# A transformer trunk on one core: units that keep three weight sums instead of two, and jobs that stand elsewhere in their stages

## The chip, the cores and the metric

The kernel runs on one core of one Trainium2 chip. The metric is the device time of one launch in microseconds, lower is better; the time before is the median of three runs. TensorE is called PE in the profile, VectorE DVE, ScalarE ACT, GpSimd POOL, and SyncE, which issues most loads, SP.

## The reference

Two layers work on 256 tokens of width 2048 in fp32. Each layer has a mixer (layer 0: neighbourhood attention with 16 heads; layer 1: a short gated convolution) and a gated MLP with a centred convolution of width 3 after the up projection (hidden width 5632).

```python
for i in range(DEPTH):
    a = rms_norm(h, mix_norm[i])
    if m == 0:
        mixed = neighborhood_attention(a, na_w_qkv[j], na_rpb[j], na_w_o[j])
    elif m == 1:
        mixed = short_conv_mixer(a, sc_w_in[j], sc_conv_w[j], sc_w_out[j])
    h = h + mixed
    h = h + conv_glu_ffn(rms_norm(h, ffn_norm[i]), ffn_w_up[i], ffn_conv_w[i],
                         ffn_conv_b[i], ffn_w_down[i])
return rms_norm(h, final_norm)

def conv_glu_ffn(x, w_up, conv_w, conv_b, w_down):
    h = dwconv_centered(x @ w_up, conv_w) + conv_b
    g, u = jnp.split(h, 2, axis=-1)
    return (jax.nn.silu(g) * u) @ w_down
```

## The kernel before, in words

**Precision.** Every fp32 operand is split into a high part (a cast, `hi`, made by ScalarE in `high_part`, L189) and a low part (the difference, `lo`, made by VectorE in `low`, L192). A product is the sum of high x high, low x high and high x low, so each weight has to be loaded, cast and subtracted before TensorE can use it.

**Stages.** The program is a list of items, each with its chunks of weights (`chunks`; a chunk is at most 128 x 1024 fp32, 512 KB). `prep_to` keeps four items' worth ahead: it loads a chunk into one of six `raw` buffers, casts it and subtracts. There are four kinds of stage:

- `Phase` (query and key, up projections, the convolution mixer's input): an item is usually two tiles of 128 output features. Its four chunks feed 32 matmuls of 512 columns on the high parts (L266) and 32 of 256 columns on the low parts (L274). Each tile is then evacuated. In an up projection that is: copy (ACT, L319), add (DVE, L320), scale (L325), convolution (ACT L333, DVE L335 twice), gate (ACT L739 or DVE L742), split for the next product (ACT L298, DVE L299). At some tiles the sums of activations for a unit are made as well (`make_forms`: POOL L520 to L523, then `split_into`, whose casts carry L298 and write `sf` and `act`).
- `Values`: the attention's value projection (L683 to L685). Between the items stand the scores (`scores`, L611 to L613 on PE, the softmax on DVE and ACT, L626 its last step) and the transposes of the probabilities (`probs`, L636).
- `Tokens` (attention output, the four half down projections, convolution output): groups of four output blocks; the weights come in pairs i, in an order written out by hand (`plan`). A pair marked P is eight products. A pair marked H is a unit: seven products (`seven`, L461 on; each product is the three matmuls L457 to L459), after Strassen. These seven need sums of weights, and their results are put together at the end of a group (`combine`, L487 on).

**Sums of weights.** The sums of a unit that can be made early are made by a job (`make`, L197) in an earlier stage: it loads three 256 KB pieces into activation tiles that are still free (the first two jobs of a stage allocate three each, later jobs alternate between the two sets), adds them on DVE (L212, L213) one chunk later, and stores the results to DRAM from ACT's queue (L218) three chunks later. Before, two sums per unit are kept. At use, `prep_to` loads them (512 KB, kind "kept"), casts them, and makes the other two sums with two dependent adds in `pair_of_sums` (L168, L169), of which the first reads the cast's source; the cast of the result waits for them.

**What sets the order.** A scheduler orders each engine's instructions at build time; each engine then runs its list in order. `load` (L157) chains every load on SP behind the one before through `newest["SP"]`, jobs' loads too. Where jobs stand is set by `QK_JOBS`, `V_JOBS`, `UP_JOBS` and `SC_JOBS` (how many per stage) and by L245 (between which items of a phase: from a fifth of the items, where the phase has introductory items, otherwise from the first, up to the share `until`).

## Time and profile before

| what | before |
|---|---|
| median of three runs | 2274.24 us (2273.21 to 2274.66) |
| the profiled execution, its time | 2272.17 us |
| its span | 2270.4 us |
| PE busy | 2205.6 us (97%) |
| DVE busy | 1862.2 us (82%) |
| ACT busy | 1305.4 us (57%) |
| mean granted clock | 0.988 |
| DMA | 524.89 MB, mean 231 GB/s |
| stores of sums (kept<-act) | 132 of 256 KB |
| loads of sums (raw<-kept) | 66 of 512 KB |

Busy time is the time in which an engine had an instruction in work. A row of the timeline gives start, duration, engine, line, shape and count, and in brackets how long the engine was idle before and what released it. The granted clock is the rate that TensorE was given; 1.00 is full.

### The profile page before, as it was taken

Reading aid. Unit: us, or ns where it says so; the run is one execution under the profiler, and the core shown is the slowest. Engines: PE = TensorE matmul, PEld = TensorE weight load, DVE = VectorE, ACT = ScalarE, POOL = GpSimd, SP = SyncE. Lnnn points to the kernel's source line nnn. Section 1 sums busy time; section 2 is a strip of 40 time slices with the busy share of each in tenths; the row PEclk is TensorE's granted clock in tenths of the full one; section 3 lists DMA queues with packets and bytes.
Section 4 is the critical chain, followed back from the end, with each engine's and each line's share of the span. In section 5 each row is a group of like instructions: output and inputs, shape, how many; then the busy total and the mean of one; then the engine's idle time right before and its main releaser. Section 6 shows DMA issues by size and latency. Waiting matters only on the chain.

```text
span 2270.4 us, 33031 instructions
## 1 busy us (share of the span) xinstructions
PE 2205.6 (97%) x11710; PEld 1897.5 (84%) x11710; DVE 1862.2 (82%) x2856; ACT 1305.4 (57%) x1991; POOL 97.1 (4%) x159
## 2 busy tenths in 40 slices
PE   9898999999999989999999999999999998999998
PEld 8787888888888778888778888878888876888886
DVE  8686777888888878888987777898888887888788
ACT  7453555566665555665655544566666654666565
POOL 0000000001000000100000000000000000000000
PEclk9999999999999999999999999999999999999999
DMA  7696746697557778755679886678965665875575
GB/s 264 206 312 229 255 158 199 232 302 246 193 175 234 246 243 258 237 193 182 217 251 314 291 272 212 205 240 282 306 196 188 209 224 204 274 244 192 172 229 161
DMA packets 347668, 524.89 MB, mean 231 GB/s; under 512 B 19824, under 2 KB 250352, under 8 KB 347504
## 3 DMA queue, kind: packets, MB, share of 16 engines
q1 hardware_dynamic: 327120, 487.55, 66.3%
q10 hardware_dynamic: 20384, 35.24, 4.1%
q8 instruction: 92, 1.51, 0.3%
q14 instruction: 72, 0.59, 0.1%
HBM read 486.01 MB, written 36.70 MB: 230 GB/s over the span
## 4 chain that ended last, share of the span: by engine, by line
PE 85%; DVE 8%; issue 3%; ACT 3%; DMA 1%; SPq 0%; ACTq 0%; DVEq 0%
PE mm L266 41%; PE mm L274 21%; PE mm L458 5%; PE mm L459 5%; PE mm L457 5%; DVE lo L192 3%; ACT hi L189 2%; PE mu L458 2%; PE mu L459 2%; PE mu L457 1%; PE mm L684 1%; PE mm L685 1%; PE mm L683 1%; DVE raw L169 1%; DVE hi L192 1%
## 5 line engine op out<-in xcount | busy, mean ns | idle before, releaser
L192 DVE TENSOR_TENSOR lo<-raw,hi 128x1024 fp32r<-128x1024 f32 (+1 forms) x858 | 1016.4, 1213 | 165.9 <-ACT hi L189 74.1
L189 ACT CAST hi<-raw 128x1024 fp32r<-128x1024 f32 (+1 forms) x924 | 907.8, 1010 | 344.7 <-DVE raw L169 120.7
L266 PE MATMUL mm<-a,hi 128*128 128x512 f32 x4096 | 976.3, 394 | 30.1 <-ACT hi L189 28.8
L266 PEld LDWEIGHTS mm<-a,hi 128*128 128x128 f32 x4096 | 766.9, 190 | 188.9 <-ACT hi L189 33.8
L274 PEld LDWEIGHTS mm<-a,lo 128*128 128x128 f32 x4096 | 513.7, 191 | 12.2
L274 PE MATMUL mm<-a,lo 128*128 128x256 f32 x4096 | 519.5, 283 | 0.0
L319 ACT COPY corr<-mm 128x256 f32<-128x256 f32 x256 | 95.1, 372 | 296.8 <-PE mm L274 292.6
L457 PE MATMUL mm<-hi,act 128*128 128x512 f32 x624 | 244.2, 393 | 2.9 <-DVE h L354 1.6
L459 PE MATMUL mm<-hi,act 128*128 128x512 f32 x624 | 243.5, 390 | 0.0
L458 PE MATMUL mm<-lo,act 128*128 128x512 f32 x564 | 220.5, 391 | 0.0
L335 DVE SCALAR_TENSOR_TENSOR conv<-pad,pt,conv 128x256 f32<-128x256 f32 x384 | 181.6, 479 | 33.0 <-ACT conv L333 25.7
L333 ACT ACTIVATE conv<-pad,pt 128x256 f32<-128x256 f32 x176 | 105.6, 601 | 119.3 <-DVE pad L325 114.8
L457 PEld LDWEIGHTS mm<-hi,act 128*128 128x128 f32 x624 | 117.6, 188 | 29.8 <-ACT hi L189 5.0
L459 PEld LDWEIGHTS mm<-hi,act 128*128 128x128 f32 x624 | 117.4, 188 | 24.4
L320 DVE TENSOR_TENSOR corr<-mm,corr 128x256 f32<-128x256 f32 x256 | 106.7, 417 | 35.3 <-ACT corr L319 34.7
L458 PEld LDWEIGHTS mm<-lo,act 128*128 128x128 f32 x564 | 106.2, 188 | 22.1
L299 DVE TENSOR_TENSOR act<-conv,act 128x256 fp32r<-128x256 f32 x88 | 37.9, 430 | 66.0 <-ACT act L298 65.9
L457 PE MATMUL mu<-hi,sf 128*128 128x512 f32 x186 | 73.4, 395 | 6.4 <-ACT hi L189 6.2
L325 DVE TENSOR_TENSOR pad<-corr,rstd 128x256 f32<-128x256 f32 x176 | 73.5, 418 | 0.6
L458 PE MATMUL mu<-lo,sf 128*128 128x512 f32 x186 | 73.6, 396 | 0.3 <-DVE lo L192 0.3
L459 PE MATMUL mu<-hi,sf 128*128 128x512 f32 x186 | 72.7, 391 | 0.0
L523 POOL TENSOR_TENSOR s<-conv 128x128 f32<-128x128 f32 x27 | 14.8, 549 | 975.3 <-DVE conv L742 975.3
(160 smaller groups left out, 1600.1 us busy)
## 6 DMA issues: line engine op xcount, KB each, us to landing
raw<-in_wup SPq DMA_DIRECT2D x352, 512.0 KB, 5.4
raw<-in_wdown SPq DMA_DIRECT2D x124, 512.0 KB, 4.2
raw<-in_wsc SPq DMA_DIRECT2D x96, 512.0 KB, 5.5
act<-in_wdown SPq DMA_DIRECT2D x156, 256.0 KB, 6.2
kept<-act ACTq DMA_DIRECT2D x132, 256.0 KB, 5.0
raw<-kept SPq DMA_DIRECT2D x66, 512.0 KB, 4.0
raw<-in_wqk SPq DMA_DIRECT2D x56, 512.0 KB, 6.5
raw<-in_wv SPq DMA_DIRECT2D x32, 512.0 KB, 5.9
```

Of the source, the lines that this page charges most:

```text
L189: newest["ACT"] = nc.scalar.copy(out=hv, in_=r)
L192: newest["DVE"] = nc.vector.tensor_sub(out=lv, in0=r, in1=hv.bitcast(F32))
L266: nc.tensor.matmul(self.ps[ft], lhsT=prepped[i][0][:, o:o + P], rhs=self.src[k], start=k == 0, stop=False)
L274: nc.tensor.matmul(self.ps[ft][:, S:], lhsT=prepped[i][1][:, o:o + P], rhs=self.src[k][:, :S], start=False, stop=k == self.nk - 1)
L319: nc.scalar.copy(out=corr, in_=ps[:, S:])
L320: nc.vector.tensor_add(out=corr, in0=ps[:, :S], in1=corr)
L325: nc.vector.tensor_mul(out=dst, in0=both(ps), in1=rstd)
L333: nc.scalar.activation(c, x[:, 1:S + 1], AF.Identity, scale=w[1], bias=b)
L335: nc.vector.scalar_tensor_tensor(out=c, in0=x[:, tap:tap + S], scalar=w[tap], in1=c, op0=ALU.mult, op1=ALU.add)
L457: nc.tensor.matmul(ps, lhsT=xh, rhs=wh, start=start, stop=False)
L458: nc.tensor.matmul(ps, lhsT=xh, rhs=wl, start=False, stop=False)
L459: nc.tensor.matmul(ps, lhsT=xl, rhs=wh, start=False, stop=stop)
```

## The change

- A job makes three sums instead of two (left + right, third piece + right, left + third piece, by three adds) and stores all three. At use, a unit loads 768 KB in two transfers: the third sum goes into the upper half of the raw buffer of the right chunk, the first two into a buffer of their own. One add then makes the one sum that is left; it reads loaded data only. `seven` uses the products in another order ("21" ahead of `b`).
- The jobs stand elsewhere: seven instead of fourteen in the attention, 44 instead of 37 in the up projections, 13 in the convolution's input. A range of items, `hosts`, takes the place of `until`: items 8 to 22 of 27 in the first half of an up projection, 3 to 16 of 22 in the second, 0 to 4 for query and key, 8 to 27 in the convolution's input.
- Loads of the attention's jobs are no longer links of the chain on SP (`strict` is false there): they follow it, and nothing is made to follow them.
- The convolution's output has four units per group instead of five, 64 in all instead of 66; the results of its first group are combined one step later.

```diff
--- before.py
+++ after.py
@@ -54,9 +54,9 @@
 S_SECOND = plan("P0 P2 H1 H3 H4 P9 H5 H6 H7 H8 P10", 0)
 S_MLP = {(0, 0): S_FIRST, (0, 1): (S_SECOND, plan("P0 P2 P5 H1 H3 H4 P9 H6 H7 H8 P10", 0)),
          (1, 0): S_FIRST, (1, 1): (plan("P0 P2 H1 H3 H4 P9 H6 H7 H8 P5 P10", 1), plan("P0 P2 H1 H3 P5 H4 H6 H7 P8 P9 P10", 0))}
-S_OUT = (plan("P0 H1 H2 P3 H4 H5 H7 P6", 0), plan("P0 P3 H1 H2 H4 H5 H7 P6", 0))
+S_OUT = (plan("P0 H1 H2 P3 H4 H5 P6 P7", 1), plan("P0 P3 H1 H2 P6 H4 H5 P7", 0))
 S_ATT = (plan("P0 P1 P2 H6 P3 H7 P4 P5", 1),) * 2
-QK_JOBS, V_JOBS, UP_JOBS, SC_JOBS = (0, 4, 4, 0), (2, 2, 2, 0), (9, 9, 11, 8), 16
+QK_JOBS, V_JOBS, UP_JOBS, SC_JOBS = (0, 2, 2, 0), (1, 1, 1, 0), (11, 13, 9, 11), 13
 
 
 HEAD = (2, 4)
@@ -144,30 +144,26 @@
                 continue
 
             if kind == "kept":
-                load(raw, src())
-                t13, low = high_part(raw)
-                t24 = pair_of_sums(raw, prepped[-1][2], prepped[-2][2])
-                low()
-                prepped.append((t13, parts(t24)))
+                t42, left, sums = prepped[-1][2], prepped[-2][2], src()
+                load(t42[:, 4 * P:], sums[:, 8 * P:])
+                load(raw, sums[:, :8 * P])
+                nc.vector.tensor_add(out=t42[:, :4 * P].rearrange("p (f c) -> p f c", f=4),
+                                     in0=t42[:, 4 * P:].rearrange("p (f c) -> p f c", f=4),
+                                     in1=left.rearrange("p (f k c) -> p k f c", f=4, c=P)[:, 1])
+                prepped.append((parts(raw), parts(t42)))
                 continue
 
             load(raw[:, :4 * w].rearrange("p (f c) -> p f c", f=4), src.rearrange("f p c -> p f c"))
             prepped.append(parts(raw[:, :4 * w].rearrange("p (f k c) -> p f k c", f=4, c=P)) + (raw,))
 
-    def load(out, in_):
+    def load(out, in_, strict=True):
 
         with ExitStack() as order:
             if "SP" in newest:
                 order.enter_context(tc.issue_after(newest["SP"].ins))
-            newest["SP"] = nc.sync.dma_start(out=out, in_=in_)
-
-    def pair_of_sums(t13, w22, left):
-
-        l = left.rearrange("p (f k c) -> p k f c", f=4, c=P)
-        t2, t4 = w22[:, :4 * P], w22[:, 4 * P:].rearrange("p (f c) -> p f c", f=4)
-        nc.vector.tensor_add(out=t2, in0=t13[:, :4 * P], in1=t2)
-        nc.vector.tensor_add(out=t4, in0=t2.rearrange("p (f c) -> p f c", f=4), in1=l[:, 1])
-        return w22
+            last = nc.sync.dma_start(out=out, in_=in_)
+        if strict:
+            newest["SP"] = last
 
     def parts(r):
 
@@ -194,28 +190,28 @@
 
     kept, newest = {}, {}
 
-    def make(w, g, i, sets):
-
-        kept[id(w), g, i] = dst = dp.tile([P, 8 * P], F32, name=f"kept{len(kept)}")
+    def make(w, g, i, sets, strict):
+
+        kept[id(w), g, i] = dst = dp.tile([P, 3, 4 * P], F32, name=f"kept{len(kept)}")
         if len(sets) < 2:
             sets.append([act_tile().bitcast(F32) for _ in range(3)])
         else:
             sets.reverse()
-        tiles = sets[-1]
-        for x, f, k in zip(tiles, (0, 4, 4), (0, 0, 1)):
+        for x, f, k in zip(sets[-1], (0, 4, 4), (0, 0, 1)):
             f, k = 8 * g + f, 2 * i + k
-            load(x.rearrange("p (f c) -> p f c", f=4), w[f:f + 4, :, k * P:(k + 1) * P].rearrange("f p c -> p f c"))
-        l, r, t = tiles
+            load(x.rearrange("p (f c) -> p f c", f=4), w[f:f + 4, :, k * P:(k + 1) * P].rearrange("f p c -> p f c"), strict)
+        l, r, t = sets[-1]
 
         def adds():
             with tc.issue_after(newest["DVE"].ins):
                 nc.vector.tensor_add(out=l, in0=l, in1=r)
-                nc.vector.tensor_add(out=t, in0=t, in1=r)
+                nc.vector.tensor_add(out=r, in0=t, in1=r)
+                nc.vector.tensor_add(out=t, in0=l, in1=t)
 
         def store():
-            for n, x in enumerate((l, t)):
+            for n, x in enumerate((l, r, t)):
                 with tc.issue_after(newest["ACT"].ins):
-                    nc.scalar.dma_start(out=dst[:, n * 4 * P:(n + 1) * 4 * P], in_=x)
+                    nc.scalar.dma_start(out=dst[:, n], in_=x)
         stores.append((len(prepped) + ADDS, adds))
         stores.append((len(prepped) + STORES, store))
 
@@ -224,16 +220,16 @@
     def plan_jobs(w, plans):
         jobs.extend((w, g, i) for g, (order, sset, _) in enumerate(plans) for i in order if i in sset)
 
-    def take(n):
+    def take(n, strict=True):
         sets = []
-        out, jobs[:] = [(*job, sets) for job in jobs[:n]], jobs[n:]
+        out, jobs[:] = [(*job, sets, strict) for job in jobs[:n]], jobs[n:]
         return out
 
     class Phase:
 
 
 
-        def __init__(self, w, fts, nk, src, evac, intro=0, step=CH, jobs=(), until=0.7):
+        def __init__(self, w, fts, nk, src, evac, intro=0, step=CH, jobs=(), hosts=(0, 1)):
             self.w, self.nk, self.src, self.evac = w, nk, src, evac
             self.ps = {}
             order = [((ft,), [(k0, k0 + step)]) for k0 in range(0, nk, step) for ft in fts[:intro]]
@@ -242,7 +238,7 @@
             odd = len(rest) % 2
             order += [(two, [(k0, k0 + CH) for k0 in range(0, nk, CH)])
                       for two in [rest[:odd]] * odd + [rest[i:i + 2] for i in range(odd, len(rest), 2)]]
-            made, lo, hi = 0, len(order) // 5 if intro else 0, int(len(order) * until)
+            made, (lo, hi) = 0, hosts
             for n, (two, ks) in enumerate(order):
                 items.append((self, two, len(chunks), ks[0][0], ks[0][0], ks[-1][1]))
                 for ft in two:
@@ -405,7 +401,7 @@
                     chunks.append((left, 2 * P, "cols"))
                     if i in kinds:
                         chunks.append((right[:, :, P:], P, "cols"))
-                        chunks.append((lambda key=(id(w), g, i): kept[key], 8 * P, "kept"))
+                        chunks.append((lambda key=(id(w), g, i): kept[key].rearrange("p n c -> p (n c)"), 8 * P, "kept"))
                         items.append((self, g, c + 1, k, k, k + 2))
                         ends.append(c + 3)
                     else:
@@ -467,11 +463,11 @@
                 self.u = [pa.tile([P, 4 * P], F32, name="mu", tag=n) for n in ("st", "sc", "tr", "o")]
             a, e, f, b = self.u
             left = prepped[c - 1]
-            w22, (t13, t24) = prepped[c:c + 2]
+            w22, (t13, t42) = prepped[c:c + 2]
             s1, s2, s4, s3 = self.forms[i]
             raw = lambda k, t: tuple(self.src[k0 + k][:, j + t * P:j + (t + 1) * P] for j in (0, S))
             for ps, x, w, j in ((a, raw(0, 0), left, 0), ("11", raw(1, 0), left, 1), ("12", s4, w22, 0),
-                                (e, s1, t13, 0), (f, s3, t13, 1), (b, s2, t24, 0), ("21", raw(1, 1), t24, 1)):
+                                (e, s1, t13, 0), (f, s3, t13, 1), ("21", raw(1, 1), t42, 0), (b, s2, t42, 1)):
                 wh, wl = (y[:, j * 4 * P:(j + 1) * 4 * P] for y in w[:2])
                 if ps in self.u:
                     self.product(ps, *x, wh, wl, first, last)
@@ -841,7 +837,7 @@
             lo = half * HALF
             Phase(wup[layer], [f for j in range(lo, lo + HALF) for f in (2 * j, 2 * j + 1)], KT, a,
                   up_evac(layer, act, forms, S_MLP[layer, half]), intro=0 if half else 3,
-                  jobs=take(UP_JOBS[2 * layer + half]))
+                  jobs=take(UP_JOBS[2 * layer + half]), hosts=(3, 16) if half else (8, 22))
             Tokens(down[layer, half], HALF, act, evac if half else residual, S_MLP[layer, half], forms,
                    halves=4 if half and layer else 0)
 
@@ -854,11 +850,11 @@
         plan_jobs(down[1, half], S_MLP[1, half])
     for g in range(NH // 4):
         Phase(wqk, range(8 * g, 8 * g + 8), KT, a0, qk_evac, intro=0 if g else INTRO, step=STEP,
-              jobs=take(QK_JOBS[g]))
-        Values(g, a0, take(V_JOBS[g]))
+              jobs=take(QK_JOBS[g], False), hosts=(0, 4))
+        Values(g, a0, take(V_JOBS[g], False))
     Tokens(wo, KT, oT, to_norm(1, a1), S_ATT, oforms)
     mlp(0, a1, to_norm(2, a2))
-    Phase(wsc, range(3 * KT), KT, a2, sc_evac, intro=3, jobs=take(SC_JOBS), until=0.9)
+    Phase(wsc, range(3 * KT), KT, a2, sc_evac, intro=3, jobs=take(SC_JOBS), hosts=(8, 27))
     Tokens(wscout, KT, yT, to_norm(3, a3), S_OUT, yforms)
     mlp(1, a3, last_evac())
 
```

How the order on the engines moves is shown at three places. In these rows, a number after a name tells one tile from another; `mm` are results on PSUM, `corr`, `conv` and `g` steps of an evacuation, `hi` and `lo` the parts of weights, `raw` what was loaded.

The first place is ScalarE at the start of the second up projection. Before, the end of item 0 (results `mm_7794` and `mm_7811`) and the casts of item 1:

```order
L319 COPY corr_7844<-mm_7794 128x256
L333 ACTIVATE conv_7848<-pad0_83,pt_79 128x256
L319 COPY corr_7870<-mm_7811 128x256
L739 ACTIVATE g_7852<-conv_7848 128x256
L333 ACTIVATE conv_7874<-pad1_84,pt_79 128x256
L298 CAST act_7879<-conv_7874 128x256
L189 CAST hi_7893<-raw_7891 128x1024
L189 CAST hi_7899<-raw_7897 128x1024
L218 DMA kept23_7882<-act_7883 128x512
```

In the changed kernel such a place lies behind item 3 of the same stage (results `mm_8128` and `mm_8145`), with the casts of item 4:

```order
L315 COPY corr_8178<-mm_8128 128x256
L329 ACTIVATE conv_8182<-pad0_83,pt_79 128x256
L315 COPY corr_8204<-mm_8145 128x256
L735 ACTIVATE g_8186<-conv_8182 128x256
L329 ACTIVATE conv_8208<-pad1_84,pt_79 128x256
L294 CAST act_8213<-conv_8208 128x256
L294 CAST sf_8221<-s_8216 128x3x128
L294 CAST act_8101<-s_8216 128x128
L185 CAST hi_8238<-raw_8236 128x1024
L185 CAST hi_8244<-raw_8242 128x1024
L214 DMA kept18_8226<-act_8227 128x512
```

In both, the casts of the next item's weights stand behind the whole evacuation; in the changed kernel the two casts of a unit's sums (`sf`, `act_8101`) come between as well.

The second place is TensorE in the attention, at the scores of a head and the transposes of the probabilities of another. Before:

```order
L274 MATMUL mm_1078<-a_407,lo_1058 128x256
L611 MATMUL sc_1301<-qk_1146 128x256
L612 MATMUL sc_1301<-qk_1146 128x256
L613 MATMUL sc_1301<-qk_1146 128x256
L611 MATMUL sc_1301<-qk_1146 128x256
L612 MATMUL sc_1301<-qk_1146 128x256
L613 MATMUL sc_1301<-qk_1146 128x256
L636 MATMUL tr_1443<-pt_79,s_1308 128x128 x4
L266 MATMUL mm_1240<-a_119,hi_1214 128x512
```

In the changed kernel, at the same scores:

```order
L270 MATMUL mm_1222<-a_407,lo_1204 128x256
L607 MATMUL sc_1283<-qk_1137 128x256
L608 MATMUL sc_1283<-qk_1137 128x256
L609 MATMUL sc_1283<-qk_1137 128x256
L607 MATMUL sc_1283<-qk_1137 128x256
L608 MATMUL sc_1283<-qk_1137 128x256
L609 MATMUL sc_1283<-qk_1137 128x256
L270 MATMUL mm_1239<-a_119,lo_1213 128x256
L270 MATMUL mm_1239<-a_122,lo_1213 128x256
```

Before, the scores follow the last matmul of the item that they are made from (`mm_1078`), and the transposes, which need the softmax of these scores (`s_1308`), follow the scores. In the changed kernel the scores stand in the middle of the next item (`mm_1222`, `mm_1239`), and the transposes come after an item more.

The third place is VectorE in the convolution's output, at one unit among several. Before:

```order
L192 TENSOR_TENSOR hi_14404<-raw_14402,hi_14404 128x512
L168 TENSOR_TENSOR raw_14402<-raw_14407,raw_14402 128x512
L169 TENSOR_TENSOR raw_14402<-raw_14402,raw_14375 128x512
L192 TENSOR_TENSOR lo_14410<-raw_14407,hi_14409 128x1024
L192 TENSOR_TENSOR lo_14416<-raw_14402,hi_14415 128x1024
```

In the changed kernel:

```order
L188 TENSOR_TENSOR hi_14872<-raw_14870,hi_14872 128x512
L150 TENSOR_TENSOR raw_14870<-raw_14870,raw_14843 128x512
L188 TENSOR_TENSOR lo_14880<-raw_14875,hi_14879 128x1024
L188 TENSOR_TENSOR lo_14884<-raw_14870,hi_14883 128x1024
L188 TENSOR_TENSOR lo_14890<-raw_14887,hi_14889 128x4x2x128
```

The two adds L168 and L169 have become the one add L150; the rest of the unit stays as it was.

## The prediction

> **What bounds the kernel now.** I read the page first, then the waits of the matrix engine, then the windows and the timeline around every place where it stands still. The page and the list of cores:
>
> ```profile
> PE 2205.6 (97%) x11710; PEld 1897.5 (84%) x11710; DVE 1862.2 (82%) x2856; ACT 1305.4 (57%) x1991; POOL 97.1 (4%) x159
> core 0: 2270.4 us, clock 0.988
> ```
>
> TensorE is busy 2205.6 of 2270.4 us. So 64.8 us are idle, and a mean clock of 0.988 loses about another 27 us (0.012 x 2270). These 92 us are all that another order can win; the rest goes only with matmuls. What TensorE waits for (line, releaser, us in total, times, longest):
>
> ```profile
> PE mm L266 <- ACT hi L189: 28.8, 9, 5.2
> PE tr L636 <- DVE s L626: 8.1, 2, 4.1
> PE mu L457 <- ACT hi L189: 6.9, 10, 1.5
> PE sc L611 <- ACT qk L298: 3.6, 2, 1.8
> PE mm L457 <- DVE h L354: 1.6, 2, 0.8
> PE mm L457 <- ACT hi L189: 1.3, 6, 0.2
> ```
>
> Three kinds stand here: projections that wait for the high halves of their weights (L266), the attention's scores and transposes (L611, L636), and the token products (L457). The first kind is four equal pauses, two near the start of each second up projection, and three shorter ones at stage starts. TensorE's timeline (start, us, line, shape, count, idle before and releaser); the row at 827.89 is an undisturbed one:
>
> ```profile
> 796.36 9.82 PE L266 MATMUL mm<-a,hi 128*128 128x512 f32 x32 [5.20 <-ACT hi L189]
> 815.21 9.01 PE L266 MATMUL mm<-a,hi 128*128 128x512 f32 x32 [5.20 <-ACT hi L189]
> 827.89 7.44 PE L266 MATMUL mm<-a,hi 128*128 128x512 f32 x32
> 1899.27 9.65 PE L266 MATMUL mm<-a,hi 128*128 128x512 f32 x32 [5.20 <-ACT hi L189]
> 1929.07 10.08 PE L266 MATMUL mm<-a,hi 128*128 128x512 f32 x32 [5.20 <-ACT hi L189]
> 444.12 3.92 PE L266 MATMUL mm<-a,hi 128*128 128x512 f32 x16 [2.95 <-ACT hi L189]
> 1546.69 2.11 PE L266 MATMUL mm<-a,hi 128*128 128x512 f32 x8 [2.95 <-ACT hi L189]
> 1185.03 5.30 PE L266 MATMUL mm<-a,hi 128*128 128x512 f32 x22 [1.41 <-ACT hi L189]
> ```
>
> After a pause of 5.20 us the same 32 matmuls take 9.82, 9.01, 9.65 and 10.08 instead of 7.44 us, 2.20 more on average: the clock has dropped. After 2.95 us it has not (16 matmuls in 3.92 us, half of 7.44 being 3.72). So a long pause costs 5.20 + 2.20 = 7.40 us. [...]
>
> Why 5.20 is the same each time is seen on ScalarE and VectorE before 796.36:
>
> ```profile
> 791.20 0.37 ACT L319 COPY corr<-mm 128x256 f32<-128x256 f32 x1
> 794.50 0.42 DVE L742 TENSOR_TENSOR conv<-conv,g 128x256 f32<-128x256 f32 x1
> 794.96 0.40 ACT L298 CAST act<-conv 128x256 fp32r<-128x256 f32 x1 [1.53 <-DVE conv L742]
> 795.27 1.99 ACT L189 CAST hi<-raw 128x1024 fp32r<-128x1024 f32 x2
> ```
>
> The weights had long landed. But ScalarE runs in order, and the casts of the next item's weights (L189) stand behind the whole evacuation of the item just multiplied: copy, convolution, gate, cast. Its length, not the load, is the pause. Whether a pause exists is therefore a question of the order, and the order of the changed kernel can be read.
>
> **The change part by part.**
>
> *Where the pauses stand now.* In the changed order the stage starts are free: weight casts of the first items stand ahead of the evacuations. But the same knot has moved to the first hosts of jobs in each up projection: it lies behind items 8 and 9 (from 0) of both first halves and behind 3 and 4 of both second halves. That is eight places instead of four. At four of them (the first of each pair) the evacuation also carries the sums for a unit, whose two casts now lie between. What these add is seen where they are harmless today:
>
> ```profile
> 889.63 0.43 DVE L742 TENSOR_TENSOR conv<-conv,g 128x256 f32<-128x256 f32 x1
> 891.33 0.51 ACT L298 CAST sf<-s 128x384 fp32r<-128x384 f32 x1 [0.81 <-POOL s L521]
> 891.88 0.30 ACT L298 CAST act<-s 128x128 fp32r<-128x128 f32 x1
> 892.08 1.05 ACT L189 CAST hi<-raw 128x1024 fp32r<-128x1024 f32 x1
> ```
>
> From L742 to the weight cast it is 892.08 - 889.63 = 2.45 us, against 795.27 - 794.50 = 0.77 in the plain pause: 1.68 more. So four places cost 5.20 + 1.68 + 2.20 = 9.08 each and four 7.40: 36.3 + 29.6 = 65.9 us. The short-convolution stage keeps one short knot inside; I price it as its row at 1185.03, 1.41. Together 67.3. What goes: 4 x 7.40 + 2 x 2.95 + 1.41 = 36.9. Net **+30.4 us**. The bounds: without the sums' extra 6.7 less; with the lowest and the highest of the four clock prices (1.57, 2.64) about 2.5 less or 1.8 more on the four added.
>
> *Attention.* Four jobs instead of eight run beside the query-key items, and their loads no longer chain the weight loads. Today:
>
> ```profile
> 103.41 0.38 PE L611 MATMUL sc<-qk 128*128 128x256 f32 x1 [1.82 <-ACT qk L298]
> 108.78 1.08 PE L636 MATMUL tr<-pt,s 128*128 128x128 f32 x4 [4.05 <-DVE s L626]
> 67.00:118.00 51.00, 42.55 (x212) 35.63 (x211) 32.99 (x51) 20.48 (x37) 2.95 (x3) 0.90 0.73 238
> 180.00:198.00 18.00, 12.07 (x59) 10.07 (x59) 13.66 (x24) 7.34 (x15) 1.03 (x1) 0.72 0.44 138
> ```
>
> The second pair of rows are windows (length, then busy time of PE, PEld, DVE, ACT and POOL with counts, then clock, DMA share, GB/s). Idle: 8.45 + 5.93 = 14.4 us. Clock: 51 x 0.10 + 18 x 0.28 = 10.1, of which about a fifth (14.4 of 69 us) falls into the idle and isn't lost twice: 8.0. In sum 22.4. Today the scores and the softmax's transposes follow one another on TensorE with nothing between; in the changed order each has an item's matmuls ahead of it, since its weights are cast in time. I count **-22.4 us**; the ends are the idle alone (-14.4) and idle with all of the clock (-24.5).
>
> *The unit in Tokens.* Two dependent adds between two casts become one add on what was loaded. Today ScalarE waits for L169; windows around the token pauses:
>
> ```profile
> 1503.17 3.47 ACT L189 CAST hi<-raw 128x1024 fp32r<-128x1024 f32 x4 [3.14 <-DVE raw L169]
> 740.00:778.00 38.00, 36.55 (x157) 28.73 (x156) 33.46 (x38) 22.13 (x27) 0.00 (x0) 1.00 0.74 230
> 1082.00:1094.00 12.00, 9.95 (x35) 6.63 (x34) 10.49 (x12) 8.98 (x11) 0.00 (x0) 0.89 0.78 245
> 1149.00:1164.00 15.00, 14.06 (x68) 10.87 (x67) 14.43 (x20) 10.31 (x12) 0.00 (x0) 1.00 0.93 313
> 1469.00:1525.00 56.00, 51.21 (x235) 39.99 (x234) 51.64 (x68) 34.75 (x53) 0.00 (x0) 1.00 0.65 212
> 1859.00:1881.00 22.00, 20.83 (x89) 16.12 (x88) 20.21 (x24) 12.85 (x16) 0.00 (x0) 1.00 0.75 244
> ```
>
> Idle: 1.45 + 2.05 + 0.94 + 4.79 + 1.17 = 10.4; clock 12 x 0.11 = 1.3. Idle understates a pause: a row's matmul is drawn some 0.39 us long while the next may start after 7.44 / 32 = 0.23 (the undisturbed row above), so each of the 18 waits at L457 (10 + 6 + 2 above) costs 0.16 more: 2.9. Sum 14.6. The loop that causes it, a cast waiting for an add that waits for a cast, is gone; what is late next is VectorE. It has three subtractions and two shorter operations per unit, by these rows
>
> ```profile
> 1500.52 1.21 DVE L192 TENSOR_TENSOR lo<-raw,hi 128x1024 fp32r<-128x1024 f32 x1
> 1501.65 0.68 DVE L168 TENSOR_TENSOR raw<-raw 128x512 f32<-128x512 f32 x1
> ```
>
> 3 x 1.21 + 2 x 0.68 = 5.0 us against 21 matmuls at 0.23, 4.8: nearly level, so units in a row may still lose 0.2 us each. I count **-14.6 us**, with ends of -9 (a third stays) and -18.
>
> *Two units fewer, and the traffic.* A unit does seven products of three matmuls where a plain pair does eight: two units fewer add 6 x 0.23 = **+1.4 us**. The third sum adds 64 stores and 64 loads of 256 KB, spread; and a third add per job, 0.69 us on VectorE. All of it lies beside matmuls:
>
> ```profile
> 828.05:839.16 11.11, 11.11 (x66) 9.84 (x65) 9.74 (x17) 8.24 (x12) 0.46 (x1) 1.00 1.00 365
> 939.18:950.30 11.12, 11.12 (x66) 9.85 (x65) 10.31 (x19) 6.45 (x10) 0.46 (x1) 1.00 0.75 243
> L213 DVE TENSOR_TENSOR act<-act 128x512 f32<-128x512 f32 x66 | 45.8, 694 | 3.0 <-DMA act<-in_wdown 1.5 <-DMA act<-in_wo 1.4
> ```
>
> The first is an item with a job: TensorE unbroken while 365 GB/s move. An item with a job of the new kind moves 2 MB of weights, 0.75 of pieces and 0.75 of sums, 3.67 MB in 11.1 us, 330 GB/s: below what is shown. The second has a job and a unit's sums: VectorE 10.31, with one more add 11.0 of 11.11. That cover is thin (first rival).
>
> **Sum:** 30.4 - 22.4 - 14.6 + 1.4 = -5.2 us. The profiled execution took 2272.17 us with a span of 2270.4, 2.07 under the median of 2274.24; its terms hold for the median too, so 2274.24 - 5.2 = **2269.0 us**. With the ends of the terms it runs from 2260 to 2279. A difference of about 4.5 us (0.2%) can be told from none.
>
> **The rivals.**
>
> *VectorE becomes the bound in the second halves (slower).* There now 13 and 11 jobs stand in 13 neighbouring items, so about six items in each carry a job and sums. If VectorE can't fill its waits there, the 0.81 us for POOL above and the 0.47 for ScalarE in
>
> ```profile
> 795.39 0.42 DVE L299 TENSOR_TENSOR act<-conv,act 128x256 fp32r<-128x256 f32 x1 [0.47 <-ACT act L298]
> ```
>
> such an item needs 11.0 + 0.81 + 0.47 = 12.3 us, 1.2 over its matmuls: 12 x 1.2 = 14 us, hence 2283. It decides once VectorE's need passes 11.11 us in several items in a row. For it: 10.31 today. Against: items without sums need 9.74 + 0.69 = 10.4 and give time back, and four chunks are prepared ahead.
>
> *The token pauses stay (no change or slower).* If the casts of a unit still come late, for the sums' loads or for VectorE, only some 4 of the 14.6 us come: 2280. For it: 5.0 against 4.8 us; against: only units that follow one another feel it.
>
> *The new pauses are cheaper (faster).* If the sums are done early, and the clock mostly holds, 4 x 1.68 + 8 x 2.20 = 24 us less: 2245; half of it gives 2257. For it: only four of nine waits at L266 today drop the clock. Against: all four of 5.20 us did. That the knots do not appear at all, and all of the 65.9 us stay away, I hold unlikely: the order on ScalarE is fixed, and each of the four places with the same order today paused.
>
> **How the numbers follow.** Forecast 0.62 (0.37 of it below -4.5 us, 0.22 within it, 0.03 above); cheaper pauses 0.19, all faster; VectorE's bound 0.12, all slower; token pauses that stay 0.07 (0.04 within, 0.03 slower). Faster 0.56, same 0.26, slower 0.18. The range takes the forecast's own and reaches into both sides: 2256 to 2281.
>
> **What would show it.** In the changed profile TensorE should wait eight times for some 5 to 7 us at the up projection, behind items 8 and 9 of the first halves and 3 and 4 of the second, with rows of some 9.6 us for 32 matmuls behind them, and never at a stage start; no wait of over 0.5 us at the scores and transposes; ScalarE's waits for the unit's add far below today's. Wrong would be: second-half items with jobs over 11.2 us with VectorE without idle (first rival); waits at L457's successor as many as today (second); pauses under 4 us (third).

## The result and the profile after

The changed kernel takes 2260.91 us (median of 4 runs, 2260.1 to 2261.64), the kernel before 2273.72 us in the same series: a ratio of 0.9944, 95% interval 0.9926 to 0.9961, 12.8 us less. The forecast was 5.2 us less. The profiled executions have spans of 2270.4 and 2259.5 us, 10.9 apart; the steps below are counted against these.

The page, the cores and the waits of TensorE after (line, releaser, us in total, times, longest):

```profile
PE 2197.4 (97%) x11716; PEld 1902.7 (84%) x11716; DVE 1850.5 (82%) x2842; ACT 1303.6 (58%) x1985; POOL 119.1 (5%) x155
core 0: 2259.5 us, clock 0.984
```

```profile
PE mm L262 <- ACT hi L185: 50.9, 11, 7.0
PE bc L796 <- DVE conv L794: 1.6, 1, 1.6
PE st L113 <- DVE inv L755: 1.1, 1, 1.1
PE tr L779 <- DVE h L350: 0.8, 1, 0.8
PE tr L632 <- DVE act L295: 0.7, 1, 0.7
```

One kind of wait is left, and it has grown: the projections' wait for the high halves of their weights, 50.9 us instead of 28.8 (now line 262). The scores and the token products have vanished from the list; the transposes wait 0.7 us instead of 8.1. TensorE's timeline at the eight places:

```profile
448.36 10.39 PE L262 MATMUL mm<-a,hi 128*128 128x512 f32 x32 [6.95 <-ACT hi L185]
467.83 7.45 PE L262 MATMUL mm<-a,hi 128*128 128x512 f32 x24 [5.26 <-ACT hi L185]
820.30 10.46 PE L262 MATMUL mm<-a,hi 128*128 128x512 f32 x32 [6.95 <-ACT hi L185]
839.85 5.43 PE L262 MATMUL mm<-a,hi 128*128 128x512 f32 x15 [5.26 <-ACT hi L185]
1551.41 10.14 PE L262 MATMUL mm<-a,hi 128*128 128x512 f32 x32 [6.89 <-ACT hi L185]
1570.64 4.60 PE L262 MATMUL mm<-a,hi 128*128 128x512 f32 x12 [5.26 <-ACT hi L185]
1923.00 10.37 PE L262 MATMUL mm<-a,hi 128*128 128x512 f32 x32 [6.95 <-ACT hi L185]
1942.46 7.89 PE L262 MATMUL mm<-a,hi 128*128 128x512 f32 x26 [5.26 <-ACT hi L185]
```

They come in pairs, a longer and a shorter one, two pairs per layer: the eight places that the order had shown. ScalarE at the first, with the two casts of a unit's sums (`sf`, `act<-s`) ahead of the weights:

```profile
445.32 0.41 ACT L294 CAST act<-conv 128x256 fp32r<-128x256 f32 x1 [1.53 <-DVE conv L738]
446.53 0.51 ACT L294 CAST sf<-s 128x384 fp32r<-128x384 f32 x1 [0.80 <-POOL s L517]
447.06 0.30 ACT L294 CAST act<-s 128x128 fp32r<-128x128 f32 x1
447.27 1.99 ACT L185 CAST hi<-raw 128x1024 fp32r<-128x1024 f32 x2
```

The windows of a stretch of the attention and of three token stages (length, busy time of PE, PEld, DVE, ACT, POOL with counts, clock, DMA share, GB/s):

```profile
66.00:117.00 51.00, 50.31 (x276) 43.48 (x275) 37.83 (x61) 28.67 (x52) 3.97 (x3) 1.00 0.65 212
658.60:768.80 110.20, 110.20 (x489) 91.28 (x488) 94.62 (x106) 68.88 (x77) 0.00 (x0) 1.00 0.81 265
1030.60:1143.30 112.70, 112.70 (x508) 93.59 (x507) 100.19 (x119) 75.10 (x93) 0.00 (x0) 1.00 0.81 263
1414.10:1497.70 83.60, 83.60 (x379) 69.23 (x378) 72.72 (x90) 53.72 (x70) 0.00 (x0) 1.00 0.75 248
```

TensorE is busy through whole token stages, at a granted clock of 1.00. To see where the time went, I add up what each stage loses: for every two matmuls in a row on the timeline, the distance of their starts less the median distance for that line and shape (0.227 us for 512 columns, 0.120 for 256). Idle time, slow clock and delays too short to be drawn as idle are then one number. The rows are in us:

| kernel | attention | up projections and convolution input | token stages with the end |
|---|---|---|---|
| before | 23.6 | 41.4 | 23.7 |
| after | 1.6 | 72.2 | 2.9 |
| difference | -22.0 | +30.8 | -20.8 |

With 1.4 us more for the two units fewer, the sum is -10.6 us, against the -10.9 between the spans. The change wins 43 us in two places and gives 31 back in a third.

### The profile page after: what moved, and what is told of

It reads as the page before. It is cut to its first block, busy times and chain, and to the rows that moved or that the text cites. A ratio compares the mean times of both kernels' runs of the same rounds, so it can differ in the third digit from the quotient of the medians.

```text
span 2259.5 us, 33424 instructions
## 1 busy us (share of the span) xinstructions
PE 2197.4 (97%) x11716; PEld 1902.7 (84%) x11716; DVE 1850.5 (82%) x2842; ACT 1303.6 (58%) x1985; POOL 119.1 (5%) x155
## 4 chain that ended last, share of the span: by engine, by line
PE 94%; DVE 3%; ACT 2%; issue 1%; DMA 0%; POOL 0%; SPq 0%; DVEq 0%; ACTq 0%
PE mm L262 41%; PE mm L270 20%; PE mm L454 6%; PE mm L453 6%; PE mm L455 6%; PE mu L453 3%; PE mu L454 3%; PE mu L455 3%; PE mm L679 1%; PE mm L681 1%; PE mm L680 1%; DVE conv L331 1%; PE tr L361 1%; ACT hi L185 1%; DVE lo L188 1%
## 5 line engine op out<-in xcount | busy, mean ns | idle before, releaser
L262 PE MATMUL mm<-a,hi 128*128 128x512 f32 x4096 | 979.8, 396 | 51.4 <-ACT hi L185 50.9
L453 PE MATMUL mm<-hi,act 128*128 128x512 f32 x634 | 247.4, 390 | 0.0
L455 PE MATMUL mm<-hi,act 128*128 128x512 f32 x634 | 246.8, 389 | 0.0
L519 POOL TENSOR_TENSOR s<-conv 128x128 f32<-128x128 f32 x27 | 39.6, 1468 | 1079.2 <-DVE conv L738 1079.2
L321 DVE TENSOR_TENSOR pad<-corr,rstd 128x256 f32<-128x256 f32 x176 | 73.7, 419 | 0.8
L455 PE MATMUL mu<-hi,sf 128*128 128x512 f32 x180 | 70.1, 389 | 0.0
L453 PE MATMUL mu<-hi,sf 128*128 128x512 f32 x180 | 70.1, 389 | 0.0
```

The lines of the kernel that those rows point to most:

```text
L262: nc.tensor.matmul(self.ps[ft], lhsT=prepped[i][0][:, o:o + P], rhs=self.src[k], start=k == 0, stop=False)
L321: nc.vector.tensor_mul(out=dst, in0=both(ps), in1=rstd)
L453: nc.tensor.matmul(ps, lhsT=xh, rhs=wh, start=start, stop=False)
L455: nc.tensor.matmul(ps, lhsT=xl, rhs=wh, start=False, stop=stop)
```

## The experiments

The theory: each part acts in its own stage. What TensorE waits for is decided by the order on ScalarE and VectorE, and this order by which loads are chained behind which. The rivals: the pauses in the up projections are the price of the jobs' own work (three pieces, three adds, three stores); or the token stages gain by something else than the add. The same losses per stage for all runs:

| run | median us | ratio to before (95%) | attention | up and conv input | tokens |
|---|---|---|---|---|---|
| jobs' first loads free | 2221.89 | 0.9769 (0.9754 to 0.9784) | 1.4 | 32.8 | 3.4 |
| three sums alone | 2259.94 | 0.9938 (0.9922 to 0.9955) | 27.6 | 46.1 | 2.6 |
| places alone | 2281.18 | 1.0029 (1.0018 to 1.0041) | 0.7 | 73.7 | 24.2 |
| attention alone | 2252.0 | 0.9902 (0.9887 to 0.9916) | 1.2 | 41.9 | 25.0 |
| jobs prepared early | 2217.6 | 0.9753 (0.9735 to 0.9772) | 5.8 | 25.7 | 4.4 |
| hosts as before | 2233.74 | 0.9824 (0.981 to 0.9839) | 0.7 | 45.4 | 3.8 |
| add done twice | 2278.02 | 1.0018 (1.0008 to 1.0028) | 1.6 | 71.1 | 22.2 |
| attention in the chain | 2289.81 | 1.007 (1.0055 to 1.0085) | 30.6 | 72.0 | 3.8 |
| early and one item later | 2209.84 | 0.9721 (0.9707 to 0.9736) | 1.3 | 19.4 | 5.6 |
| the same, 66 units | 2208.41 | 0.9718 (0.9701 to 0.9734) | 1.4 | 12.3 | 7.1 |
| one item later alone | 2254.52 | 0.9918 (0.9903 to 0.9932) | 1.6 | 64.6 | 2.8 |
| attention with 14 jobs | 2269.72 | 0.9981 (0.9972 to 0.9991) | 11.2 | 72.1 | 2.9 |

### The parts alone

Three sums and one add, with all jobs where they stood:

```diff
 # from the changed kernel
-QK_JOBS, V_JOBS, UP_JOBS, SC_JOBS = (0, 2, 2, 0), (1, 1, 1, 0), (11, 13, 9, 11), 13
+QK_JOBS, V_JOBS, UP_JOBS, SC_JOBS = (0, 4, 4, 0), (2, 2, 2, 0), (9, 9, 11, 8), 16
-            made, (lo, hi) = 0, hosts
+            made, lo, hi = 0, len(order) // 5 if intro else 0, int(len(order) * hosts)
 # S_OUT and all loads strict as before
```

> Three kept sums and one add, but all jobs, hosts, chains and units as in the kernel before. Theory (the token stages' 21 us belong to the unit): the token stages lose almost nothing, attention 23 us and the phases 41 us as before, about 2253 us. Rival (the token stages gain by the moved jobs and the later combine): about 2273 us.

Measured 2259.94 us. The token stages lose 2.6 us, so their whole gain belongs to the unit and its sums. The attention loses 27.6 and the phases 46.1, four and five more than before: that is the price of the third sum (its add and its store, not taken apart) where jobs stand badly.

The places alone (two sums, two adds, jobs and free attention loads of the changed kernel):

```diff
 # from the kernel before
-QK_JOBS, V_JOBS, UP_JOBS, SC_JOBS = (0, 4, 4, 0), (2, 2, 2, 0), (9, 9, 11, 8), 16
+QK_JOBS, V_JOBS, UP_JOBS, SC_JOBS = (0, 2, 2, 0), (1, 1, 1, 0), (11, 13, 9, 11), 15
 # load, make and take with strict; hosts as in the changed kernel
```

> Two kept sums and two adds as before, 66 units, but the jobs, hosts and free loads in the attention of the changed kernel (two more jobs in the convolution's input). Theory (the parts add up): attention -22, up projections +31, tokens as before, about 2283 us, slower than before. Rival (the pauses of the up projections need the third add or the third store): about 2252 us.

Measured 2281.18 us, slower than before: attention 0.7, phases 73.7, tokens 24.2. TensorE's waits show both at once:

```profile
PE mm L268 <- ACT hi L191: 50.6, 10, 7.0
PE mu L459 <- ACT hi L191: 7.5, 11, 1.5
```

The pauses of the up projections are all there (50.6 us against 50.9) with two adds and two stores: neither the third add nor the third store makes them. The attention's part alone, in the kernel before:

```diff
-QK_JOBS, V_JOBS, UP_JOBS, SC_JOBS = (0, 4, 4, 0), (2, 2, 2, 0), (9, 9, 11, 8), 16
+QK_JOBS, V_JOBS, UP_JOBS, SC_JOBS = (0, 2, 2, 0), (1, 1, 1, 0), (11, 13, 11, 8), 16
-        Values(g, a0, take(V_JOBS[g]))
+        Values(g, a0, take(V_JOBS[g], False))
 # and the same in the query-key phases
```

> The kernel before with the attention's part of the change alone: seven jobs there instead of fourteen, their loads outside the chain; the seven others go into the up projections in the places of before. Theory: the scores and transposes no longer wait, -22 us, about 2252 us. Rival (fewer jobs there are paid for in the up projections by more jobs per item): 2262 us or more.

Measured 2252.0 us: this part alone beats the whole change. The seven jobs moved (six more in the up projections, one more in the convolution's input) cost nothing there (41.9 against 41.4).

### Which half of the attention's part

```diff
 # from the changed kernel
-              jobs=take(QK_JOBS[g], False), hosts=(0, 4))
+              jobs=take(QK_JOBS[g]), hosts=(0, 4))
-        Values(g, a0, take(V_JOBS[g], False))
+        Values(g, a0, take(V_JOBS[g]))
```

> The changed kernel with the attention's job loads in the chain again, still seven jobs there. The order shows casts closer behind what they wait for at two heads (0.1 and 0.7 us of matmuls between instead of over 7). Theory (the number of jobs and the chain both matter): 6 to 12 us of the 22 come back, about 2270 us. Rival (the number alone did it): no difference, 2261 us.

Measured 2289.81 us, 28.9 more than the changed kernel and far above what I expected. The attention loses 30.6 us, seven more than before the change with twice the jobs (there with two sums per job and in the first two items of a phase, here with three sums and spread over four items), and still 3 more than the fourteen jobs with three sums in the run with the sums alone (27.6). Against the changed kernel's 1.6 us, the chain alone costs 29 us here. So with the loads in the chain, fewer jobs win nothing in these places; I had read the order's small distances (0.1 and 0.7 us of matmuls) as small waits, but they hold up heads one after another:

```profile
PE sc L607 <- ACT qk L294: 8.0, 4, 2.2
PE tr L632 <- DVE s L622: 6.4, 3, 3.1
```

The other half, fourteen jobs with free loads:

```diff
-QK_JOBS, V_JOBS, UP_JOBS, SC_JOBS = (0, 2, 2, 0), (1, 1, 1, 0), (11, 13, 9, 11), 13
+QK_JOBS, V_JOBS, UP_JOBS, SC_JOBS = (0, 4, 4, 0), (2, 2, 2, 0), (8, 9, 9, 11), 13
```

> The changed kernel with fourteen jobs in the attention as before, their loads outside the chain as changed; the up projections have seven fewer in all (8, 9, 9, 11). Theory (the chain alone makes the attention's waits; the number does not matter, since the run with the chain and seven jobs lost even more than before): the attention loses under 3 us, about 2261 us. Rival (the number of jobs has its own price): 5 us or more come back, 2266 us or more.

Measured 2269.72 us; the rival holds. The attention loses 11.2 us, mostly in small waits of the transposes for the softmax and of the scores:

```profile
PE tr L632 <- DVE s L622: 5.6, 5, 1.4
PE sc L608 <- DVE qk L295: 1.6, 2, 1.0
```

Freeing the loads is worth 12 us with fourteen jobs (23.6 to 11.2; with three sums, 27.6 to 11.2 is 16), where the spread of the jobs over the items differs as well, and the smaller number 10 more, but only once the loads are free. With the loads in the chain, the number and the spread over the items weren't taken apart, nor what exactly the jobs' adds push aside on VectorE.

### The unit's add

```diff
-                nc.vector.tensor_add(out=t42[:, :4 * P].rearrange("p (f c) -> p f c", f=4),
-                                     in0=t42[:, 4 * P:].rearrange("p (f c) -> p f c", f=4),
-                                     in1=left.rearrange("p (f k c) -> p k f c", f=4, c=P)[:, 1])
+                for _ in range(2):
+                    nc.vector.tensor_add(out=t42[:, :4 * P].rearrange("p (f c) -> p f c", f=4),
+                                         in0=t42[:, 4 * P:].rearrange("p (f c) -> p f c", f=4),
+                                         in1=left.rearrange("p (f k c) -> p k f c", f=4, c=P)[:, 1])
```

> The changed kernel with the unit's one add done twice (the same result), so VectorE has as much work per unit as before, on the new loads. Theory (the second add was what made the loop of cast, subtraction, adds and cast longer than a unit's matmuls): 12 to 20 of the token stages' 21 us come back, 2273 to 2281 us. Rival (it is the loads, the later combine or the order of the products): at most 3 us, 2261 to 2264 us.

Measured 2278.02 us, 17.1 more than the changed kernel: 19.3 us of the token stages' 20.8 come back. But they don't come back where they were won. The down projections, with the end, lose 22.0 us with the add done twice, 5 more than before the change, and the convolution's output 0.2 instead of 7.1. So the run shows that a second add brings the waits back, and the nearness of the two totals is in part luck. ScalarE's waits for the add, and two units in a row in the run with the add done twice:

```profile
ACT hi L186 <- DVE raw L151: 113.4, 52, 7.6
```

```profile
1069.66 3.47 ACT L186 CAST hi<-raw 128x1024 fp32r<-128x1024 f32 x4 [3.17 <-DVE raw L151]
1076.34 3.47 ACT L186 CAST hi<-raw 128x1024 fp32r<-128x1024 f32 x4 [3.20 <-DVE raw L151]
```

and ScalarE's waits in the changed kernel:

```profile
ACT hi L185 <- PE mm L455: 127.3, 121, 2.1
ACT hi L185 <- DVE raw L150: 23.5, 28, 4.9
```

With two adds a unit comes every 6.68 us, with 3.2 us of waiting for the add in each, just as before the change (3.14 us at 1503.17 there); with one, ScalarE mostly waits for TensorE to give a buffer back, so it is ahead. The second add, 0.69 us long, stands in a loop with three subtractions and four casts, and with it the loop is longer than a unit's 4.8 us of matmuls. Its own length is not all of the difference, though: with one add, units in a row of the first layer's second down projection come 4.94 us apart (the two adds in the rows below), 1.7 less. The scheduler also orders VectorE differently. In such a row of units, before and with the add done twice, a subtraction of 1.2 us stands right ahead of the adds (1500.52 ahead of 1501.65 in the prediction's rows, 1073.62 ahead of 1074.76 with the add done twice). In the changed kernel, the one add follows the short subtraction at once:

```profile
1067.36 0.69 DVE L188 TENSOR_TENSOR hi<-raw,hi 128x512 fp32r<-128x512 f32 x1
1068.08 0.69 DVE L150 TENSOR_TENSOR raw<-raw 128x512 f32<-128x512 f32 x1
1073.02 0.69 DVE L150 TENSOR_TENSOR raw<-raw 128x512 f32<-128x512 f32 x1
```

How much is the add and how much the order wasn't taken apart. Only the convolution's output doesn't mind the second add (0.2 us lost). Its groups have four units, never more than two in a row, which is the likely reason. With five per group and one add (the three sums alone) it loses nothing either. There, one of the two edits would have done.

### The pauses in the up projections

The theory says that they come with jobs that take new tiles (the first two of a stage): such a load follows, in the order, the evacuation that takes a tile ahead of it, and the weights are chained behind the load. First those loads alone taken out of the chain:

```diff
-            load(x.rearrange(...), w[...].rearrange("f p c -> p f c"), strict)
+            load(x.rearrange(...), w[...].rearrange("f p c -> p f c"), strict and not fresh)
 # fresh = len(sets) < 2, before the tiles are taken
```

> The changed kernel, but the loads of those jobs that allocate new tiles (the first two of each stage) are no links of the chain of loads. Theory (the eight pauses in the up projections come from the order on ScalarE alone: the weight loads are chained behind loads that wait for a tile, so their casts stand behind the evacuation): no wait of L262 for a weight cast over 1 us is left, some 70 us go, about 2191 us. Rival (the pauses are the price of the jobs' own work, three pieces and three adds in the items): the time comes back as waits elsewhere in the up projections, 2245 us or more.

Measured 2221.89 us, 39 less than the changed kernel, but not the 70 expected; it lies between the theory and its rival. The weight casts no longer stand behind the evacuation; what is left is of another kind. SyncE's queue and ScalarE around a pause of 5.6 us at 839:

```profile
816.60 2.43 SPq L164 DMA_DIRECT2D act<-in_wdown  x3
819.08 0.97 SPq L164 DMA_DIRECT2D raw<-in_wup  x2
820.10 2.63 SPq L164 DMA_DIRECT2D act<-in_wdown  x3
822.83 2.13 SPq L164 DMA_DIRECT2D raw<-in_wup  x2
834.88 1.57 SPq L164 DMA_DIRECT2D act<-in_wdown  x3
836.54 2.03 SPq L164 DMA_DIRECT2D raw<-in_wup  x4
```

```profile
843.67 1.04 ACT L185 CAST hi<-raw 128x1024 fp32r<-128x1024 f32 x1 [7.97 <-DMA raw<-in_wup]
```

The free loads came late and together: three jobs' loads with half items of weights between, and the cast then waits for the transfer. So I left the chain as it is and took the tiles earlier instead:

```diff
-            prep_to(ends[item[0]])
+            n = ends[item[0]]
+            while n < len(chunks) and chunks[n][2] == "make" and isinstance(ph, Phase):
+                n += 1
+            prep_to(n)
```

> The changed kernel with all job loads in the chain, but a job is prepared ahead of the run of its item, so its tiles are taken before that item's evacuation takes one. In the order, job loads and weight loads then alternate evenly, and the casts behind the evacuation are gone but for a copy at four places. Theory (order, and in the run with the free first loads the late jobs that came in a bunch): some 72 us of up projections and short convolution become about 8, near 2197 us. Rival (the jobs' own traffic and adds cost what was left in that run, 32 us): 2220 us or more.

Measured 2217.6 us: the phases lose 25.7 us, not 8. Four pauses of 3.4 us are left, behind the second hosts; 4.2 us more are lost in the attention, where early jobs do harm. ScalarE at one of the four:

```profile
454.06 0.51 ACT L294 CAST sf<-s 128x384 fp32r<-128x384 f32 x1 [1.65 <-POOL s L517]
454.60 0.30 ACT L294 CAST act<-s 128x128 fp32r<-128x128 f32 x1
456.20 0.60 ACT L329 ACTIVATE conv<-pad,pt 128x256 f32<-128x256 f32 x1 [1.29 <-DVE pad L321]
458.35 0.42 ACT L735 ACTIVATE g<-conv 128x256 f32<-128x256 f32 x1 [1.29 <-DVE conv L331]
458.67 1.03 ACT L185 CAST hi<-raw 128x1024 fp32r<-128x1024 f32 x1
```

The cast now stands behind the gate of the item's first tile only, but that gate is late because the casts of a unit's sums, waiting for GpSimd, hold up the convolution ahead of it (by way of VectorE, which subtracts after these casts and only then scales the tile that the convolution reads). The next run moves the hosts one item on, to where no sums are made, and leaves the attention as it was:

```diff
 # from the run before; early only where ph.w is not wqk
-QK_JOBS, V_JOBS, UP_JOBS, SC_JOBS = (0, 2, 2, 0), (1, 1, 1, 0), (11, 13, 9, 11), 13
+QK_JOBS, V_JOBS, UP_JOBS, SC_JOBS = (0, 2, 2, 0), (1, 1, 1, 0), (12, 12, 9, 11), 13
-                  hosts=(3, 16) if half else (8, 22))
+                  hosts=(4, 16) if half else (9, 22))
```

> As the run with jobs prepared early, but in the up projections and the convolution's input alone, and the first hosts one item later (9 and 4), where the item before a host carries no sums (one job more in the first half of layer 0, one fewer in the second). Theory (what was left in that run is the order again: a weight cast behind a gate that waits for the sums' work): the four pauses of 3.4 us become about 2 us and the clock holds, the attention keeps what the change won, about 2198 us. Rival (they come from the jobs' traffic or adds): 2212 us or more.

Measured 2209.84 us. The four pauses are 1.7 us, and the clock holds behind them (16 matmuls in 3.94 us; without a pause ahead, at 456.94, in 3.82):

```profile
464.37 3.94 PE L262 MATMUL mm<-a,hi 128*128 128x512 f32 x16 [1.71 <-ACT hi L185]
```

That is the order, as the theory says. But 12 us over the expectation: in the second half of layer 0, where every item from 4 to 15 has a job, a new wait stands, 10.1 us lost in that phase.

```profile
PE mm L262 <- ACT hi L185: 6.8, 4, 1.7
PE mm L270 <- DVE lo L188: 4.6, 5, 2.1
```

```profile
910.93 1.05 ACT L185 CAST hi<-raw 128x1024 fp32r<-128x1024 f32 x1 [4.57 <-PE mm L270]
912.80 1.04 ACT L185 CAST hi<-raw 128x1024 fp32r<-128x1024 f32 x1 [0.52 <-DMA raw<-in_wup]
```

```profile
912.31 0.42 DVE L295 TENSOR_TENSOR act<-conv,act 128x256 fp32r<-128x256 f32 x1 [4.12 <-ACT act L294]
912.66 1.22 DVE L188 TENSOR_TENSOR lo<-raw,hi 128x1024 fp32r<-128x1024 f32 x1
```

This is not the prediction's first rival, VectorE as the bound. VectorE stands idle for 4.12 us ahead of the late subtraction, for a cast that stands on ScalarE behind the weight cast at 910.93, and ScalarE waits for the weights. Their load was issued at 903.31, behind three loads of a job, and landed at 910.83, 0.10 us before that cast began, though the profile puts the wait down to a matmul. The next one was issued at 903.91 and landed at 912.71, 0.09 us before its cast. So the weights land late here, in items that each load for a job as well. Whether fewer jobs in a row would cure it was not tried. With 66 units:

```diff
-S_OUT = (plan("P0 H1 H2 P3 H4 H5 P6 P7", 1), plan("P0 P3 H1 H2 P6 H4 H5 P7", 0))
+S_OUT = (plan("P0 H1 H2 P3 H4 H5 H7 P6", 0), plan("P0 P3 H1 H2 H4 H5 H7 P6", 0))
 # SC_JOBS = 15
```

> The same with 66 units instead of 64 (five per group in the convolution's output, combined at once, as before). Theory: the two units win 1.4 us of matmuls and cost nothing with one add, about 2196.5 us. Rival (the changed groups were needed to keep VectorE ahead): 2200 us or more.

Measured 2208.41 us (2203.94 to 2211.08), the best of all and 52.5 us under the changed kernel; against the run before it the difference of 1.4 us is inside the spread of either. It lies beyond the rival's 2200, but the theory's number had been counted from the 2198 us expected of the run before, which took 2209.84. The convolution's output loses nothing with five units per group, which is against the rival. In the second half of layer 0, whose instructions stand in the same order in both runs, this run loses 4.0 us instead of 10.1, so the order alone does not fix what is lost there. Its page:

```profile
PE 2180.0 (99%) x11710; PEld 1888.1 (86%) x11710; DVE 1856.8 (84%) x2856; ACT 1302.3 (59%) x1991; POOL 136.2 (6%) x159
```

Two runs on where the hosts stand, with the chain as changed. The rule of before:

```diff
-            made, (lo, hi) = 0, hosts
+            made, lo, hi = 0, len(order) // 5 if intro else 0, int(len(order) * hosts)
```

> The changed kernel with the rule of before for where the jobs stand in a phase (from the first item, or from a fifth of the items, to 0.7 or 0.9), everything else as changed. Theory: the phases lose about 46 us, as in the run with the sums alone, instead of 72: about 2235 us. Rival (the later hosts are needed for the gains elsewhere): 2258 us or more.

Measured 2233.74 us: 27 us less than the changed kernel, with the phases at 45.4. The new hosts buy nothing. They are 27 of the 31 us given back; the other 4 go to the third sum, as in the run with the sums alone. And the hosts of the changed kernel one item later:

```diff
-                  hosts=(3, 16) if half else (8, 22))
+                  hosts=(4, 16) if half else (9, 22))
 # UP_JOBS (12, 12, 9, 11)
```

> The changed kernel with nothing but the first hosts one item later (9 and 4; one job moved from the second to the first half of layer 0), so that neither of the two items before a pause carries sums. Theory (the sums' casts make four of the eight pauses 1.7 us longer and the clock's loss there 1.2 us larger): eight pauses of about 5.2 us, about 11 us less, 2250 us. Rival (the longer pauses belong to the first host as such): 2258 to 2264 us.

Measured 2254.52 us, 6.4 less, by the losses 7.6: eight pauses of the same length now, at the first and the second host alike (43.7 us in nine waits).

```profile
441.20 7.44 PE L262 MATMUL mm<-a,hi 128*128 128x512 f32 x32
457.74 9.21 PE L262 MATMUL mm<-a,hi 128*128 128x512 f32 x32 [5.27 <-ACT hi L185]
```

The sums' casts do make the longer four longer, by 1.7 us each. The clock's share did not shrink as I had put it: it is about 1.7 us behind four of these pauses and 2.7 behind the other four, at one and the same length.

## Why the prediction was right, and where not

**The up projections (+30.4 forecast, +30.8 found).** The number, the places, the length of the pauses and their cause were right: eight, at items 8 and 9 and 3 and 4, 6.95 and 5.26 us against 6.88 and 5.20. The clock behind a pause cost 2.9 us at the longer and 1.8 at the shorter ones, where 2.20 was put for all; on average 2.4. The nearness of the net is in part luck: the pauses that go were put at 36.9 us and these stages lost 41.4 before, those that come at 67.3 and they lose 72.2, so both sides were short by nearly 5 us, which cancels.

The price of the clock is not a matter of a pause's length alone: behind pauses of 5.27 us it was 1.7 or 2.7 us (the run with the hosts one item later), behind the four of 5.20 us before 1.57 to 2.64. The granted clock behind these four shows where the difference lies. It was 0.50 for the first 4.9, 3.1, 4.5 and 5.4 us of matmuls (up to 801.2, 818.3, 1903.7 and 1934.5), then 1.00 again, and half of each is 2.4, 1.6, 2.2 and 2.7 us, about what was lost (2.38, 1.57, 2.21 and 2.64). Why it rose sooner behind one pause than behind another, no run shows. Nor was it lost behind long pauses alone. In the attention before, a pause of 1.97 us at 73.04 with one of 0.53 us behind it was followed, from 74.89 to 77.45, by matmuls 0.43 us apart instead of 0.23, at a granted clock of 0.50, while behind the 2.95 us at 444.12 it stayed at 1.00.

**The attention (-22.4 forecast, -22.0 found).** The size was right. Of its cause the prediction named two, fewer jobs and loads outside the chain; the chain is the one without which the other wins nothing. One transpose still waits 0.7 us, where the prediction had said none over 0.5.

**The tokens (-14.6 forecast, -20.8 found).** The mechanism was right: the loop is gone. The size is the mis-sized term, and nearly all of the error. I had added idle time in five windows, the clock, and 0.16 us for each recorded wait. By the starts of matmuls the token stages of before lose 2.9, 6.7, 7.1, 2.7 and (with the end) 4.2 us. The first four show only 1.6, 3.0, 4.7 and 1.3 us of idle over their whole length, the clock taking about 1 us more: a good third of the loss leaves no idle, because a drawn matmul (0.39 us, 0.227 from start to start) overlaps the next by 0.16 us, and a recorded wait is not made for each of these delays. The 0.16 us for each recorded wait was about right; what the sum lacks is some 40 delays of about 0.1 us each that leave no idle at all, 4 us together, and about 1 us that the last stage won. The third that "stays" and VectorE's 5.0 against 4.8 us didn't show: no token stage but the last loses more than 0.2 us.

**The two units (+1.4).** Not to be told from the times alone: 66 against 64 units in the best order differ by 1.4 us, and the times of either run spread over 4 to 7. With the losses of the table taken off, the spans are 2181.7 us before and 2182.8 after, which fits.

**The rivals.** VectorE did not become the bound in the changed kernel: behind the pauses of layer 0's second half TensorE runs unbroken through every item with a job, 11.12 us each. VectorE is at times without idle there (11.20 us busy of the 11.20 from 918.60), but the next item gives the time back (8.77 of 11.10), as the prediction argued. The token pauses did not stay, the new pauses were not cheaper.

**The range.** Added up straight, the ends of the terms give 2254 to 2284 us; the prediction's 2260 to 2279 follows only if they are added as the root of their squares, which it doesn't say.

## What to carry to other kernels

Read the order of every engine in a changed program before you run it: here a weight cast that stood behind an evacuation on ScalarE was a pause of 5.20 us before the change and of 5.26 or 6.95 after it. Before, the evacuation's last copy began at 791.20 and the item's first cast at 795.27, though the last of the item's four loads, issued at 782.40, had landed 6.7 us later. Where loads are chained for order, look for one that needs a tile which another engine takes first. What to do about it is to be tried at each place: in the up projections taking the tile earlier won more than letting its load out of the chain (25.7 against 32.8 us lost), where late loads came in a bunch; in the attention letting the loads out won the 22 us, and taking tiles earlier lost 4. Measure a loss as starts of instructions against their pitch, not as drawn idle time, and by stage: two parts that win 43 us hid one here that cost 31.

## What the runs showed that I had not expected

- Seven jobs in the chain, spread over a phase, cost the attention more than fourteen had in its first two items (30.6 against 23.6 us, or 27.6 with three sums per job).
- The clock behind pauses of the same length costs different amounts: 1.7 or 2.7 us at 5.27 us in one run, and 1.57, 2.21, 2.38 and 2.64 us at 5.20 before.
- With the pauses gone, the next wait shows at once: TensorE never waited for a subtraction in an up projection of the changed kernel; with the hosts an item later and the tiles taken early it did, for 4.6 us in all with 64 units, behind weights that landed late, and 1.5 us with 66.
